# Resident rotary tables, two swapped-copy buffers, later gate weights, and new priorities in a two-layer hybrid trunk

## The chip, the cores and the metric

The kernel runs on one core of one Trainium2 chip, in one launch. The metric is the device time of that core in microseconds; smaller is better. TensorE (PE) multiplies matrices, VectorE (DVE) and ScalarE (ACT) do elementwise work, GpSimd (POOL) and SyncE (SP) here mostly issue transfers. SP, ACT and POOL each issue DMA transfers from an instruction list that they work through in order; an instruction that waits holds everything behind it on that engine.

## The reference, cut to what matters

Two layers work on 512 latent tokens and 256 context tokens of width 1024. The second layer updates latent tokens alone.

```python
def layer_forward(x, xc, ...):
    shift, scale, gate = split(silu(c) @ w_ada + b_ada, 3)      # adaLN, also for the context
    h = rms_norm(x) * (1.0 + scale) + shift
    p = h @ w_in                                                # 6176 columns
    xbc, dt_raw, k, v, u, uv, g_a, z, q, g_c = split(p, ...)
    ya = chunk_mlp(u, uv, g_a, ...)                             # spatial gating in chunks of 128 tokens
    ys = ssd_bidir(conv_silu(xbc), softplus(dt_raw), ...)       # chunked scan, forward and backward, 16 heads
    yb = ssd_output(ys, ..., z, ...)                            # times silu(z), group RMS norm
    q, k = apply_rope(q, cos, sin), apply_rope(k, cos, sin)     # latent tokens only
    o = latent_diff_attention(q, k, v, k_ctx, v_ctx, lam)       # 4 heads, two score maps each, subtracted
    yc = diff_post(o, subln_g, lam_init, g_c)                   # RMS norm, times silu(g_c)
    return x + gate * (concatenate([ya, yb, yc]) @ w_out)

def apply_rope(t, cos, sin):
    t1, t2 = halves(t)
    return concatenate([t1 * c - t2 * s, t1 * s + t2 * c])
```

After the two layers the latent tokens get a final RMS norm.

## The kernel before, in words

Activations lie feature-major: 128 features on the partitions, the 768 tokens along the free dimension (context 0 to 255, latents 256 to 767; SEGS names the two segments). Products in 32-bit precision are made of three matmuls: the operand and the weight are each split into a rounded high part (ACT) and the rest (DVE) by `split` (L144 to L146), and high x high, high x low and low x high are added. `proj` (L370 on) makes one block of 128 output columns: 8 k-slices x 3 matmuls for each segment, at lines L387, L391 and L392. `load_w` (L357) asks for the block's weights (512 KB) on SP into one of three buffers (raw, NRAW).

A layer goes through these stages. First the modulated norm h, kept in two parts (in the first layer beside the adaLN products that it needs, whose weights wa are asked for at L265; in the second at the end of the first layer's output). Then the scan, in two groups g of eight heads: for every chunk of 128 tokens and direction, `chunk_out` asks for a broadcast Fb of the running sums (L601) and later EF (L637), forms the decay matrices on DVE and ACT (L605 to L617) and multiplies. Beside it run the projections that the attention needs: `spill_block` writes k, q and v to DRAM, k and q once more in 32-row pieces (L407) for the rotation, and the silu of g_c.

Then the attention. `roped` reads a head's block (L685) and its copy with the halves swapped (L687), multiplies them by cos and sin on DVE (L689, L690) and adds them (L691). `head_in` does so for k and q and splits them; the halves of kh and kl go through a transfer (L703, L704). For every query tile, `scores` makes two score maps (L749, L752), their minimum (L754, as the maps are negated) and exponentials (L756); `weights` subtracts and transposes (L770 to L779); `values` multiplies with v and normalises (L790 to L801). Beside the attention run the other branches: uv, z and u blocks, the group norm, the remaining adaLN columns (`ada_steps`, weights wa at L194) and the mix with wsT (L911) and bsb (L913). Then the g_a blocks and the output projection: for each token tile, four quarters of 512 mixed features, in the order KQ, the features read back as yl (L1020), multiplied at L1025 to L1027.

The order of the work is fixed before the launch. The framework takes the instructions in program order, `tc.high_priority(n)` moves the ones inside it ahead by n places, and a planner that simulates the engines by its own cost estimate sets each engine's list and the buffers. On the chip every engine follows its list. QUEUES says which engine issues which transfer (a for ACT, g for POOL, s for SP). Memory of one stage is used again by the next: cos and sin lie in the attention's pool and so are loaded in each layer (L675, L676) once the scan has left that memory. The pool has one buffer, qs, for the swapped copies. PACE ties projection blocks to the attention: the n-th block after the scan may not begin before the first score matmul of the attention unit (head and query tile) with the index

```python
i = int(PACE[li][0] + PACE[li][1] * len(paced))
mark = marks[i] if 0 <= i < len(marks) else None
```

NADA says how many adaLN steps go with each z block. NPF says from which of a head's last units on the next head is fetched. GRP is how many token tiles of the output are worked on together, QE how many of their quarters go first when there is more than one, and OWN which PSUM tiles they use.

Of the kernel before, what the change touches and what calls it, by code (L numbers as in the profile page):

```python
# [11 lines left out]
F32 = mybir.dt.float32  # L12
F32R = mybir.dt.float32r
AF = mybir.ActivationFunctionType
ALU = mybir.AluOpType
# [5 lines left out]
P = 128  # L21
DM = 1024
NL, NCX = 512, 256
# [21 lines left out]
NAH = 2  # L45
HPX = 20000
HPS = 20000
HPW = 9000
NPART = 2
NOA = 2  # L50
HPO = 9000
GRP = ((1, 1), (4, 1))
PACE = ((-8, 1.4), (-4, 0.8))
DTB = "sc"
TKD = -1
FL = 0
HPW0 = 50000
HPW1 = 14000
HPC = 12000
HPR = 0  # L60
HPR1 = 0
HPV = 0
LAG = 1
NADA = (2, 1)
WPOOL = "none"
HPM = 0
QE = (3, 3)
NY = 3
OWN = ("aaaaaooooooo", "aaooaooo")
NWA = (2, 3)  # L70
HP = 7000
HPA = 12000
HPada = 7000
HPw = 7000
HPsp = 7000
HPsi = 7000
HPcv = 7000
HPge = 7000
HPwo = 7000
HPD = 0  # L80
KQ = ((12, 4, 8, 0), (4, 8, 0, 12))
NPF = 2
NKH = 1
GEC = True
SIC = False
QUEUES = dict(st="a", s3="g", yh="a", yl="g", cs="g", fb="g", ef="g", yp="a", gc="s", r_="s", sw="s", kh="a", kl="g", gg="g", vf="s", z2="g", z1="g", zs="g", us="g", ul="a", gt="s", yo="a", xo="s", xs="s", xa="a", ou="s")
ACT_DIRS = (0, 1)
# [4 lines left out]
def tile_hybrid_trunk(ctx: ExitStack, tc: tile.TileContext, ins, out: bass.AP):  # L92
    nc = tc.nc
    act, dve, pool, pe = nc.scalar, nc.vector, nc.gpsimd, nc.tensor
    Q = {k: {"a": nc.scalar, "g": nc.gpsimd, "s": nc.sync}[v] for k, v in QUEUES.items()}

    const = ctx.enter_context(tc.tile_pool(name="const", bufs=1))
# [23 lines left out]
    for t, n in ((sel, "sel"), (ident, "ident"), (tri_u, "tri_u"), (tri_l, "tri_l"), (id2, "id2")):  # L121
        nc.gpsimd.dma_start(t, ins[n])
    dve.memset(ones, 1.0)
    mhalf = const.tile([P, 1], F32, name="mhalf")
    dve.memset(mhalf, -0.5)
# [21 lines left out]

# [1 line left out]
    class Layer:  # L149
        pass  # L150

    def params(li):
# [13 lines left out]
        L.cng4, L.sng2, L.slg2 = hal[:, 72:76], hal[:, 76:84], hal[:, 84:85]  # L166
        row = small.tile([P, 320], F32, tag="row", name=f"row{li}")
        nc.sync.dma_start(row, ins["row"][li : li + 1, :].to_broadcast([P, 320]))
# [4 lines left out]
        lamt = small.tile([P, 2], F32, tag="lamt", name=f"lamt{li}")  # L173
        lpj = small.tile([P, 64], F32, tag="lpj", name=f"lpj{li}")
        for i in range(2):
# [8 lines left out]

# [1 line left out]
    def ada_steps(mp, todo):  # L186
        """todo: (layer, its index, first of four blocks); one step for each block"""
        pend = None
        for L, li, b0 in todo:
            part = mp.tile([P, 4, P], F32, tag="part", bufs=NPART, name=f"part{li}_{b0}")  # L190
            for i in range(4):
                with tc.high_priority(HPada):
                    wa = wpool.tile([P, KD, P], F32, tag="raw", bufs=NRAW, name=f"wa{li}_{b0}_{i}")
                    nc.sync.dma_start(wa, ins["w_ada"][li, :, P * (b0 + i) : P * (b0 + i) + P].rearrange("(k p) m -> p k m", p=P))  # L194
                pa = bank("acc", f"pa{li}_{b0}_{i}")
                for k in range(KD):
                    j = k % 4
                    pe.matmul(pa[32 * j : 32 * j + 32, :P], sc[:, k, :], wa[:, k, :], start=k < 4, stop=k >= 4)
                act.activation(part[:, i, :], pa[:, :P], AF.Copy)
                if pend:  # L200
                    ada_second(mp, *pend)
                    pend = None
                yield
            pend = L, li, b0, part
        ada_second(mp, *pend)
# [21 lines left out]

# [1 line left out]
    def modulate(L, li, t, xa, xb, rs):  # L229
# [21 lines left out]
    def first_layer_in(L, sp, sx, ws, w_split):  # L251
        """norm and modulation of the inputs by feature blocks, the first projections beside it"""
        xn = [sx.tile([P, 3, DM], F32, tag="xT", bufs=2, name=f"xn{i}") for i in range(2)]
# [5 lines left out]
        def ada_in(k):  # L259
            """shift and scale of feature block k"""  # L260
            with tc.high_priority((HPW0, HPW1, HPW)[min(k, 2)] if FL else HPW):
# [81 lines left out]
    for li in range(DEPTH):  # L343
# [12 lines left out]

# [1 line left out]
        def load_w(c0, n, name):  # L358
# [52 lines left out]
        def silu_block(c0, name):  # L411
            """2 * silu of a projected block"""
            res = proj(c0, lat_only, name)
# [15 lines left out]
        def finish(kt, y, t3=t3):  # L429
            """a finished block of the mixed features, in two parts"""  # L430
            hi = t3(f"yhi{li}_{kt}", dt=F32R)
            lo = t3(f"ylo{li}_{kt}", dt=F32R)
            split(hi[:, tl0:], lo[:, tl0:], y[:, tl0:])
            Q["yh"].dma_start(ydr[0, kt, :, tl0:], hi[:, tl0:].bitcast(F32))
            Q["yl"].dma_start(ydr[1, kt, :, tl0:], lo[:, tl0:].bitcast(F32))

        # ================= SSD =================
        with tc.tile_pool(name=f"ssd{li}", bufs=1, reuse_waits="tile") as sp, tc.tile_pool(name=f"ssx{li}", bufs=1, reuse_waits="tile") as sx, tc.tile_pool(name=f"ps_s{li}", bufs=3, space=PSUM, reuse_waits="tile") as ps2:
# [32 lines left out]
            def seg_proj(w, s, tag, name):  # L471
                """three passes of one block's product over one segment"""
                o, n = SEGS[s]
# [31 lines left out]
            with tc.high_priority(HPD):  # L505
# [46 lines left out]
                Q["cs"].dma_start(ecd, ecT)  # L552

            h3 = lambda a: a.rearrange("p (h q) -> p h q", q=64)
            for g in range(2):
# [24 lines left out]
                def state(t, d, H_in):  # L580
                    """state after chunk t in direction d"""
                    xw = sp.tile([P, 512], F32, tag="xw", bufs=2, name=f"xw{li}_{g}_{t}_{d}")
# [74 lines left out]

            # projections that are kept for the attention
            for h in range(4):
# [5 lines left out]

        # ================= attention; beside it the other branches' gates =================
        with ExitStack() as zstack, ExitStack() as mstack, ExitStack() as astack:
# [4 lines left out]
            ps2 = astack.enter_context(tc.tile_pool(name=f"ps_a{li}", bufs=1, space=PSUM, reuse_waits="tile"))  # L672
            cos = tpa.tile([P, NL], F32, name=f"cos{li}")
            sin = tpa.tile([P, NL], F32, name=f"sin{li}")
            nc.sync.dma_start(cos, ins["cos"])  # L675
            nc.sync.dma_start(sin, ins["sin"])  # L676

# [3 lines left out]
            def roped(idx, lonly, name):  # L681
                """a head's projected block, both parts of it, latents rotated"""
                o0 = NCX if lonly else 0
                r_ = a3(f"qr{name}", tag="rk", bufs=NRK)
                Q["r_"].dma_start(r_[:, o0:], kq3[idx, 4:8, :, o0:])  # L685
                sw = tpa.tile([P, NL], F32, tag="qs", bufs=1, name=f"qs{name}")
                Q["sw"].dma_start(sw, kq3[idx, 1::3, :, NCX:NT])  # L687
# [44 lines left out]
            def scores(H, h, t):  # L732
                """exponentials of one query tile's two (negated, scaled) score maps, their sums"""
                nk = NT if t > 1 else NCX
# [26 lines left out]
            def weights(H, h, t, Es):  # L761
                """difference of the two maps, transposed"""
                nm = f"{li}_{h}_{t}"
# [63 lines left out]

# [1 line left out]
            def z3(name, dt=F32):  # L829
# [35 lines left out]

# [1 line left out]
            wsT = mp.tile([P, 4, P], F32, name=f"wsT{li}")  # L867
            nc.gpsimd.dma_start(wsT, ins["wsT"][li])
            bsb = mp.tile([P, 512], F32, name=f"bsb{li}")
            nc.gpsimd.dma_start(bsb, ins["chunk_bs"][li : li + 1, :].to_broadcast([P, 512]))  # L870
            dve.tensor_scalar(bsb, bsb, 0.25, None, ALU.mult)
            vtok = mp.tile([P, TT - t0, 512], F32, name=f"vtok{li}")

            def gelu2_block(c0, name):
                """2 * gelu of a projected block"""
                res = proj(c0, lat_only, name)
# [58 lines left out]
            for g in range(2):  # L935
                sacc = None
                for j in range(4):
                    kt = 4 * g + j
                    zg = silu_block(C_Z + P * kt, f"z{li}_{kt}")
                    if kt == TKD:  # L940
# [33 lines left out]
        with tc.tile_pool(name=f"outa{li}", bufs=1, reuse_waits="tile") as oa, tc.tile_pool(name=f"outb{li}", bufs=1, reuse_waits="tile") as op, tc.tile_pool(name=f"ps_o{li}", bufs=NOA, space=PSUM, reuse_waits="tile") as ps2:  # L974
# [7 lines left out]

            # ================= output projection, gated residual =================
            if not upd:
# [4 lines left out]
            for n in range(2):  # L989
# [20 lines left out]
                def product(t, qs):  # L1010
                    """part of one token tile's product"""
                    own = OWN[li][len(order) * n + order.index(t)] == "o"
# [115 lines left out]
```

## Time and profile before

| | |
|---|---|
| time, three runs | 1450.55, 1453.93, 1457.49 us; median 1453.93 |
| profiled execution | span 1448.3 us from the first to the last instruction; its own time is not listed apart from the runs |
| instructions | 21208 |
| mean granted TensorE clock | 0.964 |
| moved by DMA | 255.97 MB, mean 177 GB/s |

In the views, times are in us from the span's start. A window gives for each engine its busy time and the number of instructions, then the granted clock (1.00 is 2.4 GHz, and half of it the other level, so a mean between them is a mixture), the mean busy share of the DMA engines, and what they moved. PE's matmuls overlap: the mean duration of one is longer than the distance to the next. A wait is put down to what came last.

### The profile page before, as it was taken

The page shows a single profiled execution, that of the slowest core. Times are in us where ns is not written, and L with a number is a line of the kernel's source. Part 1 is how long each engine was busy: PE and PEld are TensorE (multiplying, and loading weights), DVE is VectorE, ACT ScalarE, POOL GpSimd, SP SyncE. Part 2 cuts the span into 40 slices and gives each one's busy share as a digit, 9 for nine tenths or more (in the row PEclk, how much of TensorE's full clock was granted, in tenths as well). Part 3 has the DMA queues.
Part 4 walks back from the last instruction along what each step waited for, and adds up shares of the span by engine and source line. Part 5 has one row for each costly group of instructions (what it writes and reads, how often), then busy time and mean ns, then how long its engine had stood idle before and what let it go on. Part 6 is the DMA issues. An engine that isn't in the chain of part 4 may idle for free.

```text
span 1448.3 us, 21208 instructions
## 1 busy us (share of the span) xinstructions
PE 1337.9 (92%) x7944; PEld 1101.8 (76%) x7944; DVE 945.3 (65%) x1465; ACT 656.1 (45%) x1406; POOL 214.5 (15%) x418
## 2 busy tenths in 40 slices
PE   4999999999988999999999989999999689989987
PEld 3787888778867787788887768778778557778765
DVE  4497897587576657775232458887677477787432
ACT  3257634624455547554121235833623455575320
POOL 2002023113101113220000000202213001222000
PEclk8999999999999989999999999999999899989999
DMA  9424255745937447567878522625737954557885
GB/s 290 125 74 131 72 164 169 204 127 189 310 112 200 138 138 237 168 202 255 249 236 238 160 67 64 161 84 164 219 102 205 255 155 127 188 161 231 267 270 162
DMA packets 271782, 255.97 MB, mean 177 GB/s; under 512 B 14384, under 2 KB 223552, under 8 KB 271680
## 3 DMA queue, kind: packets, MB, share of 16 engines
q1 hardware_dynamic: 176624, 126.07, 31.1%
q0 software_dynamic: 18800, 66.68, 14.7%
q10 hardware_dynamic: 76256, 61.88, 13.9%
q8 instruction: 62, 1.02, 0.3%
q14 instruction: 40, 0.33, 0.1%
HBM read 199.12 MB, written 49.17 MB: 171 GB/s over the span
## 4 chain that ended last, share of the span: by engine, by line
PE 53%; DMA 18%; issue 12%; DVE 9%; ACT 6%; POOL 2%; SPq 1%; ACTq 0%; DVEq 0%; POOLq 0%
PE oacc L1027 4%; PE oacc L1026 4%; PE oacc L1025 4%; DMA Fb<-csd 3%; DMA yl<-ydr 3%; DMA qsq<-kq 2%; PE pS L585 2%; PE accc L387 2%; PE accc L391 2%; PE accc L392 2%; ACT Fb L608 2%; PE pO L790 2%; DMA qsk<-kq 2%; PE po L640 2%; PE acck L387 2%
## 5 line engine op out<-in xcount | busy, mean ns | idle before, releaser
L608 ACT ACTIVATE Fb<-Fb,dt_fp 128x128 f32<-128x128 f32 x320 | 98.6, 392 | 89.2 <-DVE Fb L605 89.2
L387 PE MATMUL accc<-h_hi,whic 128*128 128x512 f32 (+1 forms) x312 | 108.5, 348 | 5.5 <-ACT xp L451 3.8
L391 PE MATMUL accc<-h_lo,whic 128*128 128x512 f32 (+1 forms) x312 | 107.2, 344 | 0.0
L392 PE MATMUL accc<-h_hi,wloc 128*128 128x512 f32 (+1 forms) x312 | 106.8, 342 | 0.3 <-DVE wloc L146 0.3
L1025 PE MATMUL oacc<-wohi,yl 128*128 128x512 f32 x240 | 95.1, 396 | 5.0 <-DMA yl<-ydr 3.9
L1027 PE MATMUL oacc<-wohi,yl 128*128 128x512 f32 x240 | 95.4, 397 | 2.8 <-DMA yl<-ydr 2.8
L456 DVE SCALAR_TENSOR_TENSOR yv<-xp,hal,yv 128x772 f32<-128x772 f32 (+1 forms) x96 | 94.1, 993 | 5.7 <-ACT yv L454 4.5
L1026 PE MATMUL oacc<-wolo,yl 128*128 128x512 f32 x240 | 94.8, 395 | 1.0 <-DVE wolo L146 1.0
L756 ACT ACTIVATE Ea<-sm,mx 128x768 f32<-128x768 f32 (+1 forms) x80 | 65.2, 816 | 47.9 <-DVE mx L754 34.7
L605 DVE TENSOR_TENSOR Fb<-Fb,dt_cs 128x1024 f32<-128x1024 f32 x40 | 48.8, 1221 | 50.1 <-DMA Fb<-csd 50.0
L754 DVE TENSOR_REDUCE mx<-sm 128x1 f32<-128x768 f32 (+1 forms) x80 | 67.1, 843 | 13.6 <-PE sm L752 13.5
L387 PE MATMUL accz<-h_hi,whiz 128*128 128x512 f32 (+1 forms) x192 | 71.9, 375 | 0.8 <-DVE gtz L426 0.4
L391 PE MATMUL accz<-h_lo,whiz 128*128 128x512 f32 (+1 forms) x192 | 70.3, 366 | 0.0
L392 PE MATMUL accz<-h_hi,wloz 128*128 128x512 f32 (+1 forms) x192 | 70.1, 365 | 0.0
L387 PEld LDWEIGHTS accc<-h_hi,whic 128*128 128x128 f32 x312 | 59.4, 190 | 13.9 <-ACT xp L451 5.1
L749 PE MATMUL sm<-kh,qq 128*128 128x256 f32 (+1 forms) x144 | 52.5, 382 | 14.6 <-ACT Ea L756 12.9
L790 PE MATMUL pO<-v,wt 128*128 128x128 f32 x416 | 59.4, 295 | 6.5 <-DVE gg L801 4.8
L637 POOL DMA_DIRECT2D EF<-ecd x72 | 44.7, 627 | 139.3 <-DVE xT L642 128.3
L392 PEld LDWEIGHTS accc<-h_hi,wloc 128*128 128x128 f32 x312 | 59.5, 191 | 7.3 <-DVE wloc L146 0.5
L391 PEld LDWEIGHTS accc<-h_lo,whic 128*128 128x128 f32 x312 | 59.4, 190 | 6.8 <-issue 0.7
L790 PEld LDWEIGHTS pO<-v,wt 128*128 128x128 f32 x416 | 55.2, 207 | 11.6 <-DVE gg L801 5.5
L1043 DVE TENSOR_TENSOR go<-oacc,gate 128x512 f32<-128x512 f32 x20 | 13.7, 687 | 70.9 <-PE oacc L1027 70.9
(374 smaller groups left out, 3874.5 us busy)
## 6 DMA issues: line engine op xcount, KB each, us to landing
yl<-ydr ACTq DMA_DIRECT2D x120, 256.0 KB
wa<-in_w_ada SPq DMA_DIRECT2D x48, 512.0 KB
Fb<-csd POOLq DMA_DIRECT2D x40, 512.0 KB, 5.9
wo<-in_w_out SPq DMA_DIRECT2D x32, 512.0 KB
rawc<-in_w_in SPq DMA_DIRECT2D x22, 512.0 KB
EF<-ecd POOLq DMA_DIRECT2D x72, 128.0 KB, 3.1
rawz<-in_w_in SPq DMA_DIRECT2D x16, 512.0 KB
ydr<-yhi ACTq DMA_DIRECT2D x12, 384.0 KB
```

What stands on the lines that cost most here:

```text
L387: m = pe.matmul(acc[:, :n], hi[:, k, :], h_hi[:, k, o : o + n], start=k == 0, stop=False)
L391: pe.matmul(acc[:, :n], hi[:, k, :], h_lo[:, k, o : o + n], start=False, stop=False)
L392: pe.matmul(acc[:, :n], lo[:, k, :], h_hi[:, k, o : o + n], start=False, stop=k == KD - 1)
L456: dve.scalar_tensor_tensor(yv[:, lo_:], xp[:, lo_ + tap : tap + W2], L.convh[:, j, tap : tap + 1], yv[:, lo_:], ALU.mult, ALU.add)
L608: act.activation(Fb[:, h, :], Fb[:, h, :], AF.Exp, bias=fp[:, o : o + 1])
L749: m = pe.matmul(c_, H.qs[i][:, tsl], H.kh[i][:, k0 : k0 + kn], start=True, stop=False)
L754: dve.tensor_reduce(mx[:, i : i + 1], smap[:, s0 : s0 + nk], AX.X, ALU.min)
L756: act.activation(Es[i], smap[:, s0 : s0 + nk], AF.Exp, bias=mx[:, i : i + 1], scale=-1.0, accum_out=z[:, i, t % 2 : t % 2 + 1])
L790: pe.matmul(o_, H.w[:, k, P * ql : P * ql + P], H.v[:, k, :], start=k == 0, stop=k == nkt - 1)
L1025: pe.matmul(accs[t], yh[0][:, k, :], whi, start=q == 0 and k == 0, stop=False)
L1026: pe.matmul(accs[t], yh[0][:, k, :], wlo, start=False, stop=False)
L1027: pe.matmul(accs[t], yh[1][:, k, :], whi, start=False, stop=q == 3 and k == 3)
```

## The change

`cos` and `sin` move to the pool that lives through the whole kernel and are asked for once, on POOL, where the first layer's scan begins. Two parameter tiles of each layer get one buffer in place of two. The swapped copies get two buffers (NQS). wsT and bsb are asked for in `mix_in`, called before block z4. Three kinds of transfer change their queue: s3 and fb from POOL to SP, ul from ACT to SP. The other constants are new values for priorities (HP...), pace, prefetch and the output's order; some act on nothing here, as HPW0, HPW1 and HPC, which are read only if FL is set. Comments are dropped.

```diff
-HPX = 20000
+HPX = 28500
-HPW = 9000
+HPW = 0
-HPO = 9000
-GRP = ((1, 1), (4, 1))
-PACE = ((-8, 1.4), (-4, 0.8))
+HPO = 26000
+GRP = ((2, 1), (4, 1))
+PACE = ((-8, 1.4), (-10, 0.3))
-HPW0 = 50000
+HPW0 = 49000
-HPC = 12000
-HPR = 0
-HPR1 = 0
+HPC = 11000
+HPR = 2000
+HPR1 = 3000
-NADA = (2, 1)
+NADA = (2, 0)
-QE = (3, 3)
+QE = (0, 3)
-OWN = ("aaaaaooooooo", "aaooaooo")
+OWN = ('aaaaaoooaooo', 'aaoooaoo')
-HPA = 12000
-HPada = 7000
-HPw = 7000
+HPA = 26000
+HPada = 6000
+HPw = 26000
-HPcv = 7000
+HPcv = 10700
-KQ = ((12, 4, 8, 0), (4, 8, 0, 12))
-NPF = 2
+KQ = ((12, 4, 8, 0), (0, 4, 8, 12))
+NPF = 1
+NQS = 2
+MIXLATE = True
-QUEUES = dict(st="a", s3="g", ..., fb="g", ..., ul="a", ...)
+QUEUES = dict(st="a", s3="s", ..., fb="s", ..., ul="s", ...)
...
+    cos = const.tile([P, NL], F32, name="cos")
+    sin = const.tile([P, NL], F32, name="sin")
...
-        row = small.tile([P, 320], F32, tag="row", name=f"row{li}")
+        row = small.tile([P, 320], F32, tag="row", bufs=1, name=f"row{li}")
...
-        lpj = small.tile([P, 64], F32, tag="lpj", name=f"lpj{li}")
+        lpj = small.tile([P, 64], F32, tag="lpj", bufs=1, name=f"lpj{li}")
...
+            if li == 0:
+                nc.gpsimd.dma_start(cos, ins["cos"])
+                nc.gpsimd.dma_start(sin, ins["sin"])
             h3 = lambda a: a.rearrange("p (h q) -> p h q", q=64)
...
-            cos = tpa.tile([P, NL], F32, name=f"cos{li}")
-            sin = tpa.tile([P, NL], F32, name=f"sin{li}")
-            nc.sync.dma_start(cos, ins["cos"])
-            nc.sync.dma_start(sin, ins["sin"])
...
-                sw = tpa.tile([P, NL], F32, tag="qs", bufs=1, name=f"qs{name}")
+                sw = tpa.tile([P, NL], F32, tag="qs", bufs=NQS, name=f"qs{name}")
...
             wsT = mp.tile([P, 4, P], F32, name=f"wsT{li}")
-            nc.gpsimd.dma_start(wsT, ins["wsT"][li])
             bsb = mp.tile([P, 512], F32, name=f"bsb{li}")
-            nc.gpsimd.dma_start(bsb, ins["chunk_bs"][li : li + 1, :].to_broadcast([P, 512]))
-            dve.tensor_scalar(bsb, bsb, 0.25, None, ALU.mult)
+
+            def mix_in():
+                nc.gpsimd.dma_start(wsT, ins["wsT"][li])
+                nc.gpsimd.dma_start(bsb, ins["chunk_bs"][li : li + 1, :].to_broadcast([P, 512]))
+                dve.tensor_scalar(bsb, bsb, 0.25, None, ALU.mult)
+
+            if not MIXLATE:
+                mix_in()
...
                     kt = 4 * g + j
+                    if kt == 4 and MIXLATE:
+                        mix_in()
```

## Rows read from the trace of the kernel before

**Rows 1.** The page, part 1: busy time of each engine, its share, instructions.
```profile
PE 1337.9 (92%) x7944; PEld 1101.8 (76%) x7944; DVE 945.3 (65%) x1465; ACT 656.1 (45%) x1406; POOL 214.5 (15%) x418
```

**Rows 2.** Windows of 25 us: length; PE, PEld, DVE, ACT, POOL busy; clock; DMA; GB/s.
```profile
25.00:50.00 25.00, 22.54 (x178) 16.67 (x178) 11.26 (x34) 5.33 (x11) 0.17 (x3) 0.66 1.10 269
...
400.00:425.00 25.00, 20.71 (x114) 16.85 (x113) 18.61 (x36) 13.29 (x32) 0.00 (x0) 0.86 0.42 126
...
450.00:475.00 25.00, 21.16 (x145) 15.92 (x146) 14.12 (x29) 10.14 (x28) 2.43 (x4) 0.86 0.54 144
...
500.00:525.00 25.00, 22.37 (x135) 19.48 (x134) 13.91 (x27) 11.61 (x26) 3.71 (x5) 0.73 0.62 176
...
700.00:725.00 25.00, 25.00 (x112) 20.66 (x112) 3.30 (x5) 2.17 (x6) 0.00 (x0) 1.00 0.77 225
...
1375.00:1400.00 25.00, 20.50 (x78) 15.91 (x77) 11.31 (x14) 8.08 (x13) 0.00 (x0) 0.86 0.90 280
```

**Rows 3.** The same columns for longer stretches, by stage.
```profile
200.00:380.00 180.00, 175.07 (x1125) 147.90 (x1124) 134.09 (x184) 78.05 (x201) 45.23 (x69) 1.00 0.63 190
...
850.00:1120.00 270.00, 262.28 (x1535) 218.95 (x1534) 210.99 (x290) 128.46 (x272) 49.01 (x109) 1.00 0.47 133
...
1125.00:1175.00 50.00, 32.66 (x168) 23.95 (x167) 24.35 (x36) 18.41 (x33) 1.07 (x2) 0.80 0.72 195
1175.00:1325.00 150.00, 138.90 (x802) 113.99 (x801) 121.24 (x208) 93.43 (x208) 35.80 (x62) 0.97 0.57 174
```

**Rows 4.** Timeline of SP, layer 1: start, duration, engine, line, operation, tiles, count.
```profile
1116.80 0.42 SPq L724 DMA_DIRECT2D vf<-vd  x1
1117.27 1.39 SPq L675 DMA_DIRECT2D cos<-in_cos  x1
...
1122.86 8.29 SPq L676 DMA_DIRECT2D sin<-in_sin  x1
...
1139.69 0.53 SPq L687 DMA_DIRECT2D qsq<-kq  x1
```

**Rows 5.** Timeline of DVE, same stretch; in brackets the idle time before and its releaser.
```profile
1135.32 0.69 DVE L690 TENSOR_TENSOR qrk<-qrk,cos 128x512 f32<-128x512 f32 x1 [8.64 <-DMA cos<-in_cos]
...
1137.59 0.68 DVE L689 TENSOR_TENSOR qsk<-qsk,sin 128x512 f32<-128x512 f32 x1
...
1147.78 0.69 DVE L689 TENSOR_TENSOR qsq<-qsq,sin 128x512 f32<-128x512 f32 x1 [1.92 <-DMA qsq<-kq]
...
1166.50 0.69 DVE L689 TENSOR_TENSOR qsq<-qsq,sin 128x512 f32<-128x512 f32 x1 [5.60 <-DMA qsq<-kq]
```

**Rows 6.** Timeline of PE, same stretch.
```profile
1133.75 1.54 PE L729 MATMUL pvt<-ident,vf 128*128 128x128 f32 x6 [3.89 <-DMA vf<-vd]
...
1151.83 0.80 PE L749 MATMUL sm<-kh,qq 128*128 128x256 f32 x2 [1.58 <-DVE qq L710]
...
1169.14 0.58 PE L749 MATMUL sm<-kh,qq 128*128 128x256 f32 x1 [6.96 <-ACT Ea L756]
```

**Rows 7.** Timeline of DVE in layer 0.
```profile
458.96 0.69 DVE L689 TENSOR_TENSOR qsq<-qsq,sin 128x512 f32<-128x512 f32 x1 [4.28 <-DMA qsq<-kq]
...
466.51 0.69 DVE L689 TENSOR_TENSOR qsk<-qsk,sin 128x512 f32<-128x512 f32 x1 [3.81 <-DMA qsk<-kq]
```

**Rows 8.** The tile wsT: durations min/median/max, first and last start.
```profile
L911 PE MATMUL pmx<-wsT,vtok x80: 270/275/377, 607.3 to 1311.1; 128*128 128x128 f32 x80
```

**Rows 9.** Waits of all engines: who waited for whom, us in total, times, longest.
```profile
DVE Fb L605 <- DMA Fb<-csd: 50.0, 22, 7.5
...
POOL Fb L601 <- DVE Fb L617: 38.6, 10, 9.1
...
POOL Fb L601 <- PE py L621: 37.5, 14, 4.6
...
POOL kq L407 <- ACT spk L403: 31.8, 4, 25.5
...
ACT whiz L145 <- DMA rawz<-in_w_in: 19.3, 7, 6.1
```

More of the change, by code (lines that the diff above doesn't have):

```diff
@@ L80 @@
 HPD = 0
-KQ = ((12, 4, 8, 0), (4, 8, 0, 12))
-NPF = 2
+KQ = ((12, 4, 8, 0), (0, 4, 8, 12))
+NPF = 1
 NKH = 1
+NQS = 2
+MIXLATE = True
 GEC = True
 SIC = False
-QUEUES = dict(st="a", s3="g", yh="a", yl="g", cs="g", fb="g", ef="g", yp="a", gc="s", r_="s", sw="s", kh="a", kl="g", gg="g", vf="s", z2="g", z1="g", zs="g", us="g", ul="a", gt="s", yo="a", xo="s", xs="s", xa="a", ou="s")
+QUEUES = dict(st="a", s3="s", yh="a", yl="g", cs="g", fb="s", ef="g", yp="a", gc="s", r_="s", sw="s", kh="a", kl="g", gg="g", vf="s", z2="g", z1="g", zs="g", us="g", ul="s", gt="s", yo="a", xo="s", xs="s", xa="a", ou="s")
 ACT_DIRS = (0, 1)
```

## The prediction

> **What bounds the kernel now.** The page's engine line comes first: TensorE (PE) is busy 92% of the span, DVE 65%, ACT 45% [rows 1]. PE sets the pace, but a busy PE is not a PE at its peak, so I read the windows next and take busy time times mean granted clock as work done (the clock during the busy part is not exactly the window's mean; that is the error of this measure). In a good slice nothing is lost: 112 matmuls of 512 columns in 25 us, 0.223 us each [rows 2]. What is lost elsewhere is the window minus this product. The two scans lose little: 180 - 175.07 = 4.9 us in 200 to 380, 270 - 262.28 = 7.7 us in 850 to 1120 [rows 3]. The losses stand at the starts of the attentions. Layer 1: in 1125 to 1175 PE is busy 32.66 us at 0.80, worth 26.1 of 50 us, a loss of 23.9; the 150 us after it lose 150 - 138.90 x 0.97 = 15.3, or 5.1 per 50 us [rows 3]. The excess is 18.8 us. Layer 0: 400 to 425 loses 25 - 20.71 x 0.86 = 7.2, 450 to 475 6.8, 500 to 525 8.7 [rows 2], against the 2.6 per 25 us of that calmer stretch. In each the clock fell to its 1.2 GHz level for a part, after PE had waited.
>
> The timelines then say why. In layer 1 the table cos is asked for at 1117.27, behind the head's own loads; DVE stands 8.64 us for it until 1135.32, PE 3.89 us for the value block (asked for beside it) until 1133.75 [rows 4 to 6]. The sin issue alone holds SP for 8.29 us [rows 4]: the DMA engines are full there (1125 to 1175 as a whole: share 0.72 [rows 3]). There is one buffer for swapped copies, so q's copy is asked for only at 1139.69, when k's copy was used, and DVE takes it at 1147.78; the first scores are at 1151.83 [rows 4 to 6]. Later DVE stands 5.60 us in its fixed order for the next head's copy (1166.50), while row maxima of this head are behind it, and PE starts its next scores at 1169.14 after 6.96 us [rows 5, 6]. Layer 0 has the same pattern: in 450 to 475 DVE waits 4.28 us for a copy of q, then 3.81 us for one of k [rows 7].
>
> **The change part by part.**
>
> **cos and sin resident, two swapped copies.** Four loads of 256 KB become two, without a wait on memory that the scan still holds. In layer 1 the first DVE rotation no longer waits for cos, and q's copy is asked for beside k's. What is late next is k's data itself, in the burst of loads at the scan's end: the value block asked for at 1116.8 was there at 1133.75. If k's and q's copies, asked for by about 1116, land between 1124 (8.1 us later, as q's copy did after 1139.69) and 1133 (as late as the value block), scores follow after what lies between DVE's use of k's copy (1137.59 [rows 5]) and the scores, less those 8.1 us: 1151.83 - 1137.59 - 8.1 = 6 us. So they come at 1130 to 1139, 13 to 22 us earlier. PE gets back at most its excess of 18.8 us. Part was already covered by other work, and projections that ran in those stalls now have no stall to fill: bounds 0 and -18.8, I take -12. In layer 0 the excess of 400 to 425 and 450 to 475 is 7.2 + 6.8 - 2 x 2.6 = 8.8; bounds 0 and -9, I take -7, as the DVE waits (4.28 and 3.81 us) fall into the second of them. The smaller of the later head changes: -1, bounds -5 and +3 (the next head is fetched one unit later with NPF 1, which can expose one load of some 5 us).
>
> Cost of residence: the two loads have nothing to wait for, so they may go out in the start, where DMA is full (25 to 50: share 1.10 at 269 GB/s [rows 2]): 0.5 MB / 269 GB/s = 1.9 us. Bounds 0 and +2, I take +1.
>
> **The gate's small weights later.** wsT and bsb move from POOL's queue at the attention's start to before block z4; two DMA issues and one DVE scaling (0.42 us) per layer move along. Their first reader was at 607.3 in layer 0 [rows 8], after all eight z blocks, so the four blocks z4 to z7 of 24 matmuls at 0.223 us (21 us) or more hide the landing. Their cost is nothing; they take 0.5 MB out of the burst, counted above. Were the cover gone, the mix would wait one landing, some 8 us as q's copy took.
>
> **Pace.** In layer 1 the index int(-4 + 0.8n) ties the blocks from the fifth on to attention units 0 to 11; int(-10 + 0.3n) is below zero for all twenty, so none is tied. In the old order the z blocks could not begin before the first scores at 1151.83, which is why PE had so little to do there. This frees 16 blocks x 24 x 0.223 = 86 us of work, with attention ahead by priority. It makes the -12 above likelier; it can also leave the attention's end bare (a rival). Bounds -8 and +15, no separate term. In layer 1 the adaLN blocks also move from beside z to beside u and the end: the same 16 small matmuls each, at nothing.
>
> **Queues.** The 40 Fb broadcasts and 32 pieces of the spilled k and q go from POOL to SP, and 8 reads of umd from ACT to SP. On POOL the Fb issues stood behind EF issues that wait for DVE, and DVE waits 50.0 us for Fb [rows 9]. Free of that, scans run DVE smoother; but PE loses only 4.9 + 7.7 us in the stretches read. Bounds -10 and, if SP is held up, +54 (the slow rival); I take -2, nearest to the small loss. The Trainium skill ("DMA: Bandwidth & Descriptors", Issuing engines are not separate DMA queues) says that the issuing engine saves only the sequencer's time, as all transfers share the same DMA engines; the same page (Specifications) puts the first byte at about 1 us from POOL and 0.6 us from SP. By that 40 x 0.4 = 16 us, an estimate, come off landings that PE does not wait for, and the scan term would be 0 instead of -2. No row here shows an Fb from SP.
>
> **Priorities, output.** Weight loads and attention get 26000. ACT waited 19.3 us in all, seven times, for z weights [rows 9], and 500 to 525 is a slice of z blocks; of its excess of 8.7 - 2.6 = 6.1 I take a third, -2 (bounds -6 and +6). In layer 1's output the order of quarters begins with the block already in SBUF, and the slice 1375 to 1400 loses 25 - 20.50 x 0.86 = 7.4 [rows 2]; I take -3 (bounds -7 and +4). GRP (2, 1) with QE 0 gives the same order of steps as before; FL is 0, so HPW0, HPW1 and HPC act on nothing. The start is bound by DMA: new priorities for x and the adaLN weights, bounds -4 and +4, taken as 0.
>
> Sum: -12 - 7 - 1 + 1 - 2 - 2 - 3 = -26. From the span of 1448.3 that is 1422. The least of the three runs is 1450.55, so at least some 2 us lie around the span; the median, 1453.93, is 5.6 above it. Against the median: 1428.
>
> **The rivals.**
> *The new order closes more than these holes.* All terms near their better bounds (-18.8 - 9 - 5 - 10 - 6 - 7 = -56), z blocks free of the pace. Some would exclude each other; 50 off gives 1404. For it: PE is idle 1448.3 - 1337.9 = 110 us [rows 1], twice that. Against: most of this lies in small gaps.
> *The hole only moves.* The attention starts earlier but the untied blocks are used up before its end, or the burst of loads and not cos decides when k lands. Then the 20 us of the two starts come back as bare attention, and with the lesser terms at half, -4 + 1, it is 1451. For it: vf landed after 17 us without any table. Against: cos stood last in that burst and has nothing in front now.
> *SP becomes the brake (slower).* Fb waits for its buffers on POOL 38.6 and 37.5 us, the spilled pieces of k 31.8 us for ACT [rows 9]; these 108 us of waiting now stand in front of weight loads in SP's fixed order. It decides once a weight load goes out more than one block's PE time (24 x 0.223 = 5.4 us for one segment) after its buffer is free. If a third shows on PE, 36 us, with the scans' -2 gone: 1428 + 2 + 36 = 1466; with half of it 1484. For it: these are long waits, and EF, which waits too, stays on POOL. Against: three raw buffers run ahead, SP's own waits are mostly for those buffers, and during them an Fb issue costs nothing.
>
> **How the numbers follow.** Forecast 0.48, its own range 1412 to 1442; more 0.20 (1388 to 1412); only moved 0.14 (1446 to 1460); SP 0.18 (1461 to 1490). Half a per cent, 7 us, is about what can be told from no change: faster 0.68, same 0.14, slower 0.18. The range 1397 to 1464 leaves out a third of the second case and half of the last, about 0.16.
>
> **What would show it.** Right: no cos among DVE's releasers; the first scores of layer 1 under 25 us after k's copy is asked for; windows there at clock 0.9 or more; no wait of 4 us or more by DVE for a swapped copy; its Fb wait under 50 us. Wrong: PE or ACT waiting for raw weights for more than 40 us in the scans (SP), or the slices before the output emptier than before (moved). A gain that lies in the scans or the outputs would make the sum right for wrong reasons.

## The result and the profile after

The changed kernel takes 1435.08 us (median of four runs, 1432.65 to 1439.0); the kernel before, on the same chip, 1452.24 (1449.46 to 1457.49). The ratio is 0.9885, with a 95% interval of 0.9847 to 0.9923: 11 to 22 us faster. The forecast was 1428, with a range of its own of 1412 to 1442, in which the measured time lies.

The last column is a second execution of the very same program: the changed kernel with its old pace (e1 below) has the same instruction lists on all five engines. What two executions of one program differ by can be read from it.

| profiled execution, us | before | after | after again (e1) |
|---|---|---|---|
| span | 1448.3 | 1437.2 | 1431.3 |
| mean granted clock | 0.964 | 0.973 | 0.976 |
| T0: start to the last po matmul of layer 1's scan | 1116.0 | 1118.7 | 1113.2 |
| S: from there to layer 1's first scores | 35.8 | 31.8 | 32.6 |
| B: from the first scores to the end | 296.5 | 286.7 | 285.5 |

T0 and S are read as below: po belongs to the scan alone, sm to the attention's scores; the pair of numbers ahead of the semicolon is the first and last start. Two views of PE by tile, layer 1 of the kernel after:

```profile
L647 PE MATMUL po<-cT,H x96: 272/275/377, 1007.9 to 1118.7; 128*128 128x128 f32 x96
L752 PE MATMUL sm<-kh,qq x64: 276/387/481, 1150.5 to 1311.1; 128*128 128x256 f32 x32, 128*128 128x512 f32 x32
```

The same program repeats S within 0.8 us and B within 1.2, but T0 only within 5.5. So the gain that can be told from the spread lies behind layer 1's scan: S is 4.0 and 3.2 us shorter, B 9.8 and 11.0. Before that, nothing is won that exceeds the spread of T0 (+2.7, -2.8).

The page's engine line and the windows that answer to [rows 1 to 3], after, with one more of layer 0 (375 to 400):

```profile
PE 1320.5 (92%) x7944; PEld 1094.1 (76%) x7944; DVE 943.7 (66%) x1465; ACT 658.6 (46%) x1406; POOL 164.5 (11%) x348
```
```profile
25.00:50.00 25.00, 22.40 (x237) 16.95 (x229) 10.83 (x22) 5.60 (x10) 0.17 (x3) 0.93 1.15 277
200.00:380.00 180.00, 175.63 (x1134) 148.85 (x1133) 134.44 (x182) 78.09 (x199) 25.13 (x42) 1.00 0.66 192
375.00:400.00 25.00, 18.05 (x98) 15.33 (x97) 14.84 (x26) 10.99 (x20) 1.05 (x2) 0.80 0.88 237
400.00:425.00 25.00, 19.57 (x129) 15.48 (x128) 16.13 (x33) 14.31 (x32) 0.00 (x0) 0.85 0.52 136
450.00:475.00 25.00, 19.34 (x154) 15.37 (x152) 11.48 (x20) 8.33 (x22) 1.88 (x3) 1.00 0.65 172
500.00:525.00 25.00, 22.47 (x177) 19.84 (x176) 16.96 (x31) 14.57 (x33) 4.27 (x7) 0.97 0.81 232
850.00:1120.00 270.00, 260.98 (x1514) 217.94 (x1515) 208.10 (x285) 127.17 (x270) 25.31 (x70) 0.99 0.47 130
1125.00:1175.00 50.00, 38.66 (x198) 30.92 (x195) 31.21 (x46) 22.11 (x37) 2.15 (x4) 0.86 0.77 212
1175.00:1325.00 150.00, 140.63 (x835) 114.92 (x834) 124.33 (x210) 99.45 (x214) 35.76 (x59) 1.00 0.65 197
1350.00:1375.00 25.00, 17.01 (x64) 12.73 (x63) 9.57 (x9) 8.61 (x11) 1.19 (x3) 0.86 0.87 273
1375.00:1400.00 25.00, 23.78 (x105) 19.36 (x104) 9.98 (x12) 6.97 (x12) 0.00 (x0) 1.00 0.90 278
```

Two slices of the kernel before that [rows 2] do not have:

```profile
375.00:400.00 25.00, 24.11 (x173) 20.43 (x172) 12.81 (x24) 12.34 (x25) 1.06 (x2) 1.00 1.04 292
1350.00:1375.00 25.00, 24.64 (x108) 19.69 (x107) 8.15 (x8) 7.14 (x8) 1.12 (x2) 1.00 0.90 270
```

PE does the same 7944 matmuls in 17.4 us less busy time, as fewer of them fall into stretches of the lower clock: busy time times mean clock is 1290 us before and 1285 after, nearly the same. In the prediction's measure (window minus busy time times clock): 1125 to 1175 loses 50 - 38.66 x 0.86 = 16.8 where it lost 23.9, and 1175 to 1325 loses 9.4 where it lost 15.3, now wholly at 2.4 GHz. Layer 0 shows no such thing: 400 to 425 loses 8.4 (7.2 before), 450 to 475 5.7 (6.8), 500 to 525 3.2 (8.7). And 375 to 400 loses 10.6 where it lost 0.9 (8.4 in the second execution): there the change opened a hole. At 385.88 PE waits 5.23 us for a uv product that stands in ACT's list behind the split of the rotated k, and DVE had waited 3.51 us for k's swapped copy. The layer's attention as a whole (365 to 685) loses 44.6 us, 37.8 in the second execution and 36.9 before. The scans gain nothing: they lose 4.4 and 11.6 (4.9 and 7.7). 1350 to 1375, which lost 0.4 before, loses 10.4; 1375 to 1400 loses 1.2 instead of 7.4: that hole moved forward.

### The profile page after: what moved, and what is told of

Its sections match the earlier page's. It is cut to its first block, busy times and chain, and to the rows that moved or that the text cites. A ratio compares the mean times of both kernels' runs of the same rounds, so it can differ in the third digit from the quotient of the medians.

```text
span 1437.2 us, 21182 instructions
## 1 busy us (share of the span) xinstructions
PE 1320.5 (92%) x7944; PEld 1094.1 (76%) x7944; DVE 943.7 (66%) x1465; ACT 658.6 (46%) x1406; POOL 164.5 (11%) x348
## 3 DMA queue, kind: packets, MB, share of 16 engines
q1 hardware_dynamic: 220336, 150.72, 37.8%
q10 hardware_dynamic: 75104, 59.26, 13.6%
q8 instruction: 62, 1.02, 0.3%
## 5 line engine op out<-in xcount | busy, mean ns | idle before, releaser
L612 DVE TENSOR_TENSOR Fb<-Fb,dt_cs 128x1024 f32<-128x1024 f32 x40 | 48.9, 1223 | 61.8 <-DMA Fb<-csd 61.6
L391 PEld LDWEIGHTS accc<-h_hi,whic 128*128 128x128 f32 x312 | 59.9, 192 | 14.1 <-ACT xp L455 7.2
L793 PE MATMUL pO<-v,wt 128*128 128x128 f32 x416 | 55.8, 283 | 6.8 <-ACT wt L782 5.8
L150 DVE TENSOR_TENSOR wolo<-wo,wohi 128x1024 fp32r<-128x1024 f32 x32 | 38.7, 1223 | 33.3 <-ACT wohi L149 33.3
L1035 PEld LDWEIGHTS oacc<-wohi,yl 128*128 128x128 f32 x240 | 45.6, 190 | 18.6 <-DMA yl<-ydr 8.3
L793 PEld LDWEIGHTS pO<-v,wt 128*128 128x128 f32 x416 | 51.8, 195 | 10.3 <-ACT wt L782 6.2
```

The lines of the kernel that those rows point to most:

```text
L391: m = pe.matmul(acc[:, :n], hi[:, k, :], h_hi[:, k, o : o + n], start=k == 0, stop=False)
L612: dve.tensor_tensor(Fb, Fb, bc8(cs, t, d, P), ALU.min)
L793: pe.matmul(o_, H.w[:, k, P * ql : P * ql + P], H.v[:, k, :], start=k == 0, stop=k == nkt - 1)
L1035: pe.matmul(accs[t], yh[0][:, k, :], whi, start=q == 0 and k == 0, stop=False)
```

## Where layer 1's first scores come from now

The answers to [rows 4 to 6], after: SP, POOL, DVE, PE and ACT at the start of the attention.

```profile
1117.56 0.68 SPq L688 DMA_DIRECT2D qrk<-kq  x1
1118.33 0.64 SPq L690 DMA_DIRECT2D qsk<-kq  x1
1119.06 2.73 SPq L688 DMA_DIRECT2D qrq<-kq  x1
1121.84 1.30 SPq L690 DMA_DIRECT2D qsq<-kq  x1
```
```profile
4.09 0.57 POOL L559 DMA_DIRECT2D cos<-in_cos  x1
...
1116.12 1.65 POOL L957 DMA_DIRECT2D yz<-ysp  x3
1118.38 0.54 POOL L957 DMA_DIRECT2D yz<-ysp  x1 [0.61 <-PE po L647]
1119.27 0.54 POOL L874 DMA_DIRECT2D wsT<-in_wsT  x1 [0.36 <-PE po L647]
```
```profile
1132.67 0.69 DVE L693 TENSOR_TENSOR qrk<-qrk,cos 128x512 f32<-128x512 f32 x1 [9.52 <-DMA qrk<-kq]
...
1136.87 0.68 DVE L692 TENSOR_TENSOR qsk<-qsk,sin 128x512 f32<-128x512 f32 x1
...
1138.80 0.68 DVE L692 TENSOR_TENSOR qsq<-qsq,sin 128x512 f32<-128x512 f32 x1
...
1156.28 0.69 DVE L692 TENSOR_TENSOR qsq<-qsq,sin 128x512 f32<-128x512 f32 x1 [0.61 <-DMA qsq<-kq]
```
```profile
1133.23 1.11 PE L907 MATMUL pv<-ident,geuv 128*128 128x128 f32 x4 [8.21 <-ACT geuv L892]
...
1150.45 0.51 PE L752 MATMUL sm<-kh,qq 128*128 128x256 f32 x2 [0.30 <-DMA kh<-kh]
```
```profile
1131.63 1.06 ACT L149 ACTIVATE whiuv<-rawuv 128x1024 fp32r<-128x1024 f32 x1 [7.71 <-DMA rawuv<-in_w_in]
...
1141.63 0.47 ACTq L706 DMA_DIRECT2D kh<-kh  x1
```

The table and the second copy do what the code says. cos is asked for at 4.09, and q's copy is asked for at 1121.84 instead of 1139.69 [rows 4] and used at 1138.80, 9 us sooner [rows 5]. But k, asked for at 1117.56, is used only at 1132.67, after a wait of 9.52 us: about as long as the wait for cos had been (8.64). Other loads of the burst at the scan's end are late now, no longer cos. wsT is still in that burst: its new place in the program changed its place in POOL's list by four reads, and it went out at 1119.27. A uv weight is late in the same burst: ACT waits 7.71 us to round it, the uv product that PE needs stands behind it in ACT's list, and so PE waits 8.21. From k on, the rotated k is split, and its second part kh goes out at 1141.63 and lands just ahead of the first scores at 1150.45, 8.8 us later. Before, that transfer (asked for at 1143.08) lay beside the wait for q's copy and its split, and q ended last [rows 6].

But PE stands only 0.30 us for kh: it works from 1133.23 on, on two uv blocks and smaller products that its list has ahead of the scores and that end there too. An earlier kh would have brought at most 0.30 us in this list. What sets S is the work ahead of the scores and PE's waits in it. These are 8.5 us now, nearly all for the uv weight, and were 11.1 before: 3.89 for the value block and 1.58 for the split q [rows 6], 0.82 for a uv product, and 4.81 for another uv product that stands behind the rotation with q's copy in DVE's list (PE, before):

```profile
1149.13 1.12 PE L899 MATMUL pv<-ident,geuv 128*128 128x128 f32 x4 [4.81 <-DVE geuv L890]
```

The hole behind the first scores is nearly closed, where DVE stood 5.60 us for the next head's copy of q and PE 6.96 us [rows 5, 6]. DVE waits 0.61 us for that copy now (and 2.63 for k's), PE 2.71. The same 24 us, before and then after:

```profile
1152.00:1176.00 24.00, 17.05 (x79) 11.99 (x80) 12.42 (x18) 8.63 (x17) 0.00 (x0) 0.78 0.47 119
```
```profile
1152.00:1176.00 24.00, 21.76 (x97) 17.96 (x98) 17.70 (x28) 10.55 (x18) 1.65 (x3) 0.93 0.65 170
```

Busy times clock goes from 13.3 to 20.2: 6.9 us of B's 9.8. That the second buffer does this is not shown. e3 below is the same kernel with one buffer; DVE waits 2.38 and 4.00 us for these two copies there, yet PE has z blocks to do meanwhile, and the 24 us from e3's first scores (1162.9) come to 22.24 x 0.93 = 20.7:

```profile
1162.90:1186.90 24.00, 22.24 (x98) 17.49 (x98) 13.56 (x22) 9.27 (x18) 0.57 (x1) 0.93 0.40 107
```

## The experiments

Each ran beside the kernel before, in five rounds. Differences in us below are differences of ratios times 1452; the ratio of after is itself known to 5.5 us on either side, and e1 gives it a second time. The theories: **P**, the pace freed the z blocks; **C**, tables and copies are the cause, whatever stands around them; **L** (the expectations call it theory B; column B below is the stage), the burst of loads sets the first scores, so fewer loads in it bring time; **N**, NADA's second value; **R**, each edit makes the planner set another order for all later work, so parts do not add. R was written down only after e1 to e4 had run. "After" or "before" says which kernel was edited.

| | from | ratio to before (95%) | median | T0 | S | B |
|---|---|---|---|---|---|---|
| before | | 1 | 1452.24 | 1116.0 | 35.8 | 296.5 |
| after | | 0.9885 (0.9847 to 0.9923) | 1435.08 | 1118.7 | 31.8 | 286.7 |
| e1 pace back | after | 0.988 (0.9845 to 0.9915) | 1433.81 | 1113.2 | 32.6 | 285.5 |
| e2 pace alone | before | 1.0049 (1.0025 to 1.0073) | 1458.21 | 1117.4 | 41.1 | 301.9 |
| e3 one copy | after | 1.0108 (1.007 to 1.0146) | 1467.66 | 1127.3 | 35.6 | 299.8 |
| e4 tables back | after | 1.0135 (1.0098 to 1.0172) | 1472.0 | 1130.1 | 53.1 | 289.0 |
| e5 tables, copies alone | before | 1.0118 (1.0097 to 1.0139) | 1466.26 | 1125.2 | 33.1 | 306.6 |
| e6 gate weights early | after | 0.9943 (0.9924 to 0.9962) | 1440.97 | 1121.1 | 34.5 | 288.5 |
| e7 queues back | after | 0.9946 (0.9926 to 0.9965) | 1441.58 | 1116.5 | 31.2 | 289.4 |
| e8 priorities back | after | 0.9983 (0.9959 to 1.0007) | 1447.32 | 1107.6 | 28.7 | 299.6 |
| e9 NADA back | after | 1.0013 (0.9987 to 1.0038) | 1451.66 | 1116.5 | 29.3 | 303.7 |
| e10 NADA alone | before | 1.0051 (1.0031 to 1.0071) | 1458.58 | 1115.6 | 36.4 | 306.3 |
| e11 late loads | after | 1.0061 (1.003 to 1.0092) | 1458.77 | 1119.0 | 27.7 | 310.5 |
| e12 the rest alone | before | 0.9979 (0.9959 to 0.9998) | 1449.16 | 1112.2 | 43.5 | 291.8 |

T0, S and B are of one profiled execution each; after's is the slowest of its four runs, e7's the quickest of its six, and e8's the quickest of its twelve (1437.67 to 1457.39). The ranges that were expected held in e1 (C), e6, e9, e10 and e12 (R, and in e9 N's too); e5, e8 and e11 came out above R's, e2, e3 and e4 above those of both theories, e7 between the two.

**e1.** `PACE = ((-8, 1.4), (-10, 0.3))` to `((-8, 1.4), (-4, 0.8))`.

> The changed kernel with layer 1's pace put back to (-4, 0.8), nothing else. The changed kernel took 1435 us, the kernel before 1452. Theory P (the gain is the untied z and u blocks, which fill PE in layer 1's attention): most of the gain goes, 1446 to 1453, and the z blocks again take some 90 us from first to last instead of 73. Theory C (the gain is the tables and the second buffer, which take DVE's waits away): 1433 to 1438, z blocks near 75 us.

The instruction lists are the same, and so is the time. P falls: in this order the ties do not bind.

**e2.** The same edit the other way, in the kernel before.

> The kernel before with layer 1's pace set to (-10, 0.3), nothing else. Theory P: 1436 to 1443, most of the 17 us without any of the rest. Theory C: 1450 to 1454, as the blocks have nothing to fill while DVE waits for tables and copies.

7 us slower. Untied blocks do not help where the pace does bind.

**e3.** `NQS = 2` to `1`.

> The changed kernel with one buffer for swapped copies (NQS 1). Theory C: 1442 to 1448, with DVE's waits for copies of q back at 20 us or more. Theory P: 1434 to 1438; the copies wait, but PE has z blocks to do meanwhile.

32 us slower than after. DVE's waits for q's copies in the whole run, after and then e3 (total, times, longest):

```profile
DVE qsq L692 <- DMA qsq<-kq: 11.8, 6, 2.9
```
```profile
DVE qsq L692 <- DMA qsq<-kq: 25.0, 7, 6.2
```

The wait comes back, as C says; but 13 us of waiting on DVE do not add up to 32, the hole behind the first scores stays closed (above), and the loss is in T0 and B as well as in S.

**e4.** `cos = const.tile(...)` back to `tpa.tile(...)` in each layer, loaded on SP as before.

> The changed kernel with cos and sin loaded in each layer's attention memory on SP again. Theory C, as the prediction had it: first scores of layer 1 at 1160 or later and 1441 to 1447. Theory B (the burst of loads at the scan's end sets when k's data land, the tables only ride in it): 0.5 MB more per layer at some 270 GB/s, at most 2 us each, 1435 to 1439.

36 us slower, 21 of them in S. SP asks for cos at 1142.03, behind the head's own blocks; the first rotation is at 1156.41, and later DVE stands for the next head's copy, with the product that PE is to have first behind it in its list (SP, then DVE, then PE, of e4):

```profile
1142.03 4.37 SPq L677 DMA_DIRECT2D cos<-in_cos  x1
```
```profile
1174.74 0.69 DVE L691 TENSOR_TENSOR qsq<-qsq,sin 128x512 f32<-128x512 f32 x1 [7.69 <-DMA qsq<-kq]
...
1176.49 0.69 DVE L897 SCALAR_TENSOR_TENSOR geuv<-gquv,geuv 128x512 f32<-128x512 f32 x1
```
```profile
1177.23 1.11 PE L906 MATMUL pv<-ident,geuv 128*128 128x128 f32 x4 [15.92 <-DVE geuv L897]
...
1183.19 0.40 PE L751 MATMUL sm<-kh,qq 128*128 128x256 f32 x2
```

With the rest of the change around them, the resident tables shorten S by as much as the prediction said (13 to 22). But DVE never stands for cos there: the rotation at 1156.41 has no wait before it. What is long is the order in which DVE's and PE's lists put the first head, the second head's copies and the uv blocks.

**e5.** The kernel before with the tables in `const`, NQS 2 and single parameter buffers, nothing else.

> The kernel before with the resident tables, two buffers for swapped copies and the two single parameter buffers, and none of the rest. Theory C (tables and copies take DVE's waits away, and that is worth 30 us and more as in the two runs that undid them): 1415 to 1428. Theory R (each edit makes the planner set another order of the whole later work, and the constants were found for one such order; what an edit removes by itself is small): anywhere from 1435 to 1460, not below 1432.

17 us slower than before. C falls as stated: S is only 2.7 us shorter, and T0 and B are 9 and 10 longer. SP asks for q's copy right behind k, its copy and q, as in after, and even sooner behind the scan's end (0.8 us, where after has 3.1), and still DVE waits (SP, then DVE, of e5):

```profile
1123.98 0.57 SPq L686 DMA_DIRECT2D qrk<-kq  x1
...
1126.03 0.53 SPq L688 DMA_DIRECT2D qsq<-kq  x1
...
1133.96 10.82 SPq L362 DMA_DIRECT2D rawz<-in_w_in  x1
```
```profile
1148.16 0.69 DVE L690 TENSOR_TENSOR qsq<-qsq,sin 128x512 f32<-128x512 f32 x1 [7.52 <-DMA qsq<-kq]
```

The copy of 256 KB is there 22 us after it was asked for, and PE waits 9.92 us for the value block asked for beside it; two buffers don't help when the transfer itself is late.

**e6.** `MIXLATE = True` to `False`.

> The changed kernel with wsT and bsb asked for where they were before (MIXLATE False). In the changed kernel wsT still goes out at 1119.27, at the head of the attention, so the load's time hardly moves. Theory C: 1433 to 1438, no change. Theory R: the planner's order differs, so 1440 to 1460, for a load that nothing waits for.

8 us slower, although the load hardly moves: it goes out at 1121.64, 0.5 us after the last po, where after has it 0.6 us behind it, now ahead of the four reads of yz. The load's own time is hardly the cause; whether it is the reads behind it was not tested.

**e7.** `s3="s", fb="s", ul="s"` to `s3="g", fb="g", ul="a"`.

> The changed kernel with Fb and the spilled pieces on POOL and umd's read on ACT again. The prediction's term (the move is worth 2 us, bounds -10 and +54): 1434 to 1440 with DVE's wait for Fb at 50 us instead of 61.6. Theory R: 1442 to 1460, and the difference lies in the attention and not in the scans.

9 us slower than after, 3 to 4 of them in B by the profiles, the rest not located (its profiled execution is no longer than after's). The view of waits, after and then e7:

```profile
DVE Fb L612 <- DMA Fb<-csd: 61.6, 22, 7.6
```
```profile
DVE Fb L612 <- DMA Fb<-csd: 46.2, 21, 6.3
```

DVE waits longer for Fb from SP than from POOL; e12 and e3 (SP) show the same beside e5 (POOL). The kernel is faster with it all the same.

**e8.** HPX, HPW, HPO, HPR, HPR1, HPA, HPada, HPw and HPcv to their old values.

> The changed kernel with nine priorities put back (x, adaLN weights, output, parameters, attention, weights, convolution). The prediction's term (2 us for weights earlier): 1435 to 1439. Theory R: the order changes less here than in the other runs (fewest lines of each engine's list move), so a smaller step, 1437 to 1446.

14 us slower, with no instruction more or less. The spread of the runs is wide; why is open.

**e9, e10.** `NADA = (2, 0)` to `(2, 1)` in after; the other way in before.

> The changed kernel with one adaLN step beside each z block of layer 1 again (NADA (2, 1)). In all runs with (2, 0) so far layer 1's z blocks took 73 to 80 us from first to last, with (2, 1) 90 to 103. Theory N (the eight adaLN loads of 512 KB each, beside z, take DMA time from the attention's start and z's own weights; without them the z blocks run closer together, and this is the gain): 1445 to 1453, z blocks 88 us or more. Theory R (the order of the whole, no single part): 1437 to 1460, z blocks as before or after, no rule.

> The kernel before with NADA (2, 0) and nothing else. Theory N: 1436 to 1444, z blocks 80 us or less. Theory R: 1448 to 1465; the z blocks may close up, but the work moved out of them comes back in the u blocks or at the end.

In after, the old value costs 19 us, as much as the whole change brings. In before, the new value costs 7. N falls: what the value does depends on what stands around it, and the z blocks, which N expected at 88 us or more in e9 and 80 or less in e10, take 85 and 84. The same adaLN steps run in all four, at other places.

**e11.** wsT, bsb and the reads of yz for z1 to z3 are tied behind the first score matmul:

```diff
-                nc.gpsimd.dma_start(wsT, ins["wsT"][li])
+                after(nc.gpsimd.dma_start(wsT, ins["wsT"][li]))
...
+                    if 1 <= kt <= 3:
+                        after(m)
```

> The changed kernel with wsT, bsb and the reads of yz for z1 to z3 tied behind the first score matmul in the planner, so that POOL issues them after kl's halves: 1.25 MB less in the burst at the attention's start. Theory B (the burst of loads sets when k and q land): first scores of layer 1 some 4 to 5 us sooner after the scan's end than 1150.5 - 1118.7 = 32 us, and 1427 to 1434 if nothing else moves. Theory R: the first scores may come sooner, the time is 1436 to 1455 all the same.

L is right on its point: S is 27.7, the shortest of all, and k is waited for 3.99 us instead of 9.52. Yet the run is 26 us slower, and B 24 longer. SP, DVE, PE and the window, of e11:

```profile
1137.51 5.23 SPq L690 DMA_DIRECT2D qsq<-kq  x1
1142.85 6.47 SPq L688 DMA_DIRECT2D qrk<-kq  x1
```
```profile
1128.26 0.69 DVE L693 TENSOR_TENSOR qrk<-qrk,cos 128x512 f32<-128x512 f32 x1 [3.99 <-DMA qrk<-kq]
...
1149.29 0.69 DVE L692 TENSOR_TENSOR qsk<-qsk,sin 128x512 f32<-128x512 f32 x1 [7.97 <-DMA qsk<-kq]
```
```profile
1155.46 1.11 PE L910 MATMUL pv<-ident,geuv 128*128 128x128 f32 x4 [5.96 <-ACT geuv L895]
1163.26 0.58 PE L752 MATMUL sm<-kh,qq 128*128 128x256 f32 x1 [6.68 <-ACT Ea L759]
```
```profile
1150.00:1175.00 25.00, 11.21 (x38) 8.66 (x39) 15.47 (x25) 7.92 (x15) 0.00 (x0) 0.59 0.56 147
```

The second head's copies now stand in a burst with the tied loads, which POOL issues from 1139.51 on; DVE stands 7.97 us for one in its fixed order, and PE has the hole of [rows 6] again (6.68 where it was 6.96), with the clock near its lower level. The hole ahead of the first scores became one behind them.

**e12.** The complement of e5: all constants, queues and late gate weights; tables per layer, one copy, old parameter buffers.

> The other half of the change: the kernel before with all new constants, the queues and the later small weights, but with cos and sin in each layer's attention memory, one buffer for swapped copies and two for the parameters. The tables and copies alone gave 1466, 15 us over the kernel before; all together gave 1435, 17 under. If the parts add (prediction), this half is worth -17 - 15 = -32: 1417 to 1422. Theory R (neither half is faster alone; the constants are values for the order that the planner makes with these buffers): 1448 to 1475.

3 us faster than before. e5 and e12 together are the change: +17 and -3, and the whole -17. The whole differs from the sum of its parts by 31 us. By the profiled executions, after minus e5 minus e12 plus before is -9 in S and -15 in B, far above what one program repeats.

What stands is R: five edits that neither add nor remove an instruction and do change an order (e2, e6, e8, e9, e10) move the time by 7 to 19 us, up to the size of the whole change, and the one that changes no order (e1) moves nothing. R names no wait, though: what remains open is which placement in B makes the order of after good. Its stretch 1176 to 1325 is at full clock; e12's, with the rest of the change alone, is not:

```profile
1176.00:1325.00 149.00, 138.58 (x791) 111.05 (x790) 121.55 (x207) 92.61 (x202) 38.66 (x59) 0.95 0.61 180
```

No version with another order ran faster than after.

## Why the prediction was right or wrong

**The total** (-26 forecast, -17 measured) lies in the range. The profiled spans give -11 and, in the second execution of the same program, -17. Of the prediction's five signs of being right only one came: no cos among DVE's releasers. The first scores come 32 us after k's copy is asked for (under 25), the clock in 1125 to 1175 is 0.86 (0.9 or more; 1.00 behind it), DVE waits 4.35 us for a copy (under 4) and 61.6 for Fb (under 50). One sign of "the hole only moves" came too: 1350 to 1375, ahead of the output's last part, is emptier than before.

**Tables and copies in layer 1, -12.** The waits it names are gone, the start came 3 to 4 us sooner. The step that failed is "they come at 1130 to 1139, 13 to 22 us earlier". Its upper end for k, "as late as the value block" (1133), was met: k was there at 1132.67, its copy used at 1136.87. What failed is "1151.83 - 1137.59 - 8.1 = 6 us": it followed k and q alone, as if the scores came when these were ready, and 1150.45 - 1136.87 = 13.6 us were left where 6 were priced. In these PE stood 0.30 us: it did the uv blocks ahead of the scores, after waiting 8.21 us for a uv weight that the prediction had no term for. So PE got back 2.6 us of waiting in S (11.1 to 8.5). The second hole, which the prediction read but did not price by itself, gave 6.9, though not by the second buffer as such (e3). Together with S that is 10 to 11, near the 12, partly by luck. The rival "the hole only moves" named the right cause ("the burst of loads and not cos decides when k lands"), without its result.

**Layer 0, -7.** Wrong: 400 to 425 and 450 to 475 lost as much as before (14.1 against 14.0), as DVE still waits for copies (4.35 and 2.91 us for those asked for at 457.32 and 457.96), and 375 to 400 lost 9.7 more. The layer gained nothing outside T0's spread. The step priced a wait as gone because its buffer was doubled, without asking if the transfer would be in time.

**Residence, +1; gate weights, 0.** cos went out at 4.09 as assumed, and the start is no longer. The gate weights were free, but did not leave the burst "counted above".

**Pace, no term.** "This frees 86 us of work" is wrong (e1). The index shows what the pace permits, not what the planner makes of it.

**Queues, -2.** The sign agrees with e7 (-9, within the bounds), the reason does not: the scans gain nothing, and DVE's wait for Fb is 61.6, not under 50. SP did not become the brake. It waits 69.4 us for DVE and 20.2 for PE in front of Fb issues, and ACT's wait for z weights is 18.5 (19.3 before):

```profile
SPq L608 <- DVE Fb L624: 69.4, 15, 11.6
```
```profile
ACT whiz L149 <- DMA rawz<-in_w_in: 18.5, 7, 5.4
```

The first is the SP view, the second that of all engines, both of after. Of the Trainium skill's rule cited there ("DMA: Bandwidth & Descriptors", Issuing engines are not separate DMA queues): by it the scan term would be 0, and the scans agree. What it does not price: DVE waits for Fb 58.5 to 67.6 us in the nine kernels with Fb on SP, against 45.4 to 50.0 in the five with it on POOL. So the move brought DVE more waiting, not less; whether by the place in SP's list or by issues that stand longer on SP, no run tells.

**Priorities, -2; output, -3.** 500 to 525 loses 5.5 less, as that term hoped, but 475 to 550 as a whole only 3.1. In the output the slice gains 6.2 and the one before loses 10, as PE waits for features read back:

```profile
PE oacc L1035 <- DMA yl<-ydr: 7.4, 2, 5.6
```

So that term had the wrong sign for the two slices together (+3.8), within its bounds. e8 undoes the priorities for 14 us, far from -2.

Sizing by terms fails here as such: e3, e4 and e9 each undo one edit and lose more than the whole change. That the sum came out near is luck in part. The two holes of layer 1's attention are real, and the new order has them smaller; the terms for layer 0 and for the output were wrong, and no edit brings its term by itself.

## What to carry to other kernels

Where a planner sets the order, an edit's worth is measured in the kernel in which it will stand: alone the tables and copies cost 17 us here, taking out either of them costs 32 or 36. Before pricing a wait as gone, ask when the transfer behind it is asked for and what stands in front of it; with the tables resident and two buffers q's copy was asked for 18 us sooner here and used 9 us sooner, and in e5, in the burst, it came late all the same. And run a constants-only edit for scale: where that alone moves 7 to 19 us of 1450, a one-off gain of 17 is a property of an order as much as of an idea.

## What was not expected of the hardware

An issue on SP can itself stand for microseconds. The median one takes 0.37 us, yet single ones held SP for 8.29 us (before [rows 4]), 10.82 (e5) and 6.47 (e11), and all of SP's later loads with it; over these stretches the DMA share was 1.04, 0.97 and 1.02. The clock followed PE's waits: 0.59 in the 25 us of e11 in which PE was busy 11.21, 1.00 in the 150 us of after in which no wait of PE is longer than 2.9 us.
